# Three more feed-forward pairs by seven products, in another order of products, with other planned durations

## The chip, the core and the metric

The kernel runs on one core of one Trainium2 chip. The metric is the time of one execution in microseconds (us) on the device. A core has a matrix engine (TensorE, PE in the profile, with PEld for its weight loads), VectorE (DVE), ScalarE (ACT), GpSimd (POOL) and SyncE (SP). PE reads operands from the on-chip memory SBUF and writes sums into PSUM banks. VectorE and ScalarE take the sums out of PSUM again. SP and POOL only issue transfers (DMAs) here, apart from a few small fills by POOL.

## The reference, cut to what matters

The reference is a two-layer trunk over 512 tokens of width 1024. Each layer has a mixer (attention in layer 0, mLSTM in layer 1), a cross-attention to a memory of 256 rows, and a gated feed-forward network with a short convolution. The change touches the feed-forward network alone:

```python
def conv_ffn(xn, w_up, conv_w, conv_b, w_down):
    h = causal_depthwise_conv(xn @ w_up, conv_w) + conv_b
    g, u = jnp.split(h, 2, axis=-1)
    return (jax.nn.gelu(g) * u) @ w_down
```

`w_up` is 1024 x 5632 and `w_down` is 2816 x 1024. The convolution has three taps along the tokens. In front of it stands an RMS norm of x, and the result is added to x.

## The kernel before, in words

**Tiles.** x lies transposed, as 8 tiles of 128 channels x 512 tokens. All products are made of three fp32r matmuls: a value v is split into a high part (the cast to fp32r, on ScalarE) and a low part (v minus the high part, on VectorE), and `mm3` (line 265) adds high x high, high x low and low x high. So each weight tile that arrives costs one cast on ScalarE and one subtraction on VectorE (line 259, `sub`).

**The feed-forward network** is `ffn_steps` (line 1119). The 5632 output channels of `w_up` are 44 blocks of 128. Pair p (0 to 21) is gate block p with up block 22+p. There are two ways to compute a pair:

- `plain` (line 1291) does two blocks of 8 x 3 matmuls over 512 tokens, takes each out of PSUM while it scales by the norm (line 1300), and hands it to `tail`.
- `seven` (line 1310) treats the pair as a 2 x 2 product of halves: gate and up block, the two halves of the 1024 inputs, and the two halves of the tokens. Instead of eight quarter products it does seven (p1 to p7), each of 4 x 3 matmuls over 256 tokens, on sums of weight quarters and on sums of x quarters. The sums of x (`th`, `tl`) are formed once per layer by `forms` (line 1223). The sums of weights are made by an adding DMA of POOL (`onto`, line 1318, into the tile `sa`) and by two additions of VectorE (`b2` line 1343, `b4` line 1347). The outputs are combined by ScalarE (`v`, `c11`) and by VectorE (`u2`, `u3`, `c22`, `c12`, `c21`, all by line 1381), and then `scaled` (line 1402) multiplies by the norm.

`tail` (line 1247) does convolution (`conv` on ScalarE, line 1257, and four `tap`s on VectorE, line 1264), gelu (line 1272), the product of gate and up (line 1274) and the split of the result into `ah` and `al`.

`SEVEN` (line 26) names the pairs that go by seven products. They are 13 of 22, in both layers; 0 to 3, 5, 11, 16, 20 and 21 are plain.

**The down products.** The 22 pairs form chunks of 4, 4, 4, 4 and 6. When a chunk of four is done, its 8 down blocks (4 x 3 matmuls of 512 columns each) are put on a queue (lines 1431 to 1437). A plain pair takes up to two of them and a seven-product pair up to three, by `fill()`, until the queue is empty; pair 4 takes none. The last four blocks of chunk 3 come behind pair 21, and chunk 4 after them.

**The order of the work** is made when the program is built. `Sched` (line 139) is a list planner: each operation is a task with an engine, a planned duration, dependencies, a priority and buffers that it takes or frees. In `run` (line 161), among the tasks that can start soonest on their engine, the one with the lowest priority number is issued. A result counts as there for another engine `lat` after the task's planned end. The buffers of a name are handed out strictly in the order in which the tasks that take them were added (`want`, line 164). What comes out is a fixed order for each engine, and for the DMA queue of SP as well; on the chip each engine goes through its own order and waits where something is late. The planner's durations are the constants at lines 1126 to 1128 and the numbers in the calls: n columns cost `tt(n)` on VectorE and `act(n)` on ScalarE, `STT` is a tap, `ACV` a convolution start. A product counts 1.42 us and 0.7 us go to each three matmuls of 512 columns. Buffers of interest are `raw` (3 weight tiles as loaded), `sa` (3), `h` (3 split weight tiles), `hs` (2 rows of a pair before the convolution), `c` (1), and `u2`, `u3`, `v` (1 each).

A plain pair takes two `raw` tiles. A seven-product pair takes one, along with one `sa`, one `sb` and one `ra`.

Of the kernel before, what the change touches and what calls it, by code (L numbers as in the profile page):

```python
# [13 lines left out]
ALU = mybir.AluOpType  # L14
# [8 lines left out]
NPAIR = DFF // P  # L23
CHUNKS = [(0, 4), (4, 4), (8, 4), (12, 4), (16, 6)]

SEVEN = (4, 6, 7, 8, 9, 10, 12, 13, 14, 15, 17, 18, 19)
EPS = 1e-6

X_AT, X_STEP = 2.6, 0.6
# [30 lines left out]
class Plan:  # L60
# [11 lines left out]
    def add(self, fn, dur=0.0, deps=(), prio=None, take=(), free=(), chain=(), pre=(), after=0.0, order=(), load=(), st=None):  # L72
        it = Item(fn, dur, [d for d in deps if d is not None], len(self.items) if prio is None else prio, take, free, chain, pre, after, order, load, st)
        it.n = len(self.items)
        self.items.append(it)
        return it
# [62 lines left out]
class Sched:  # L139
# [5 lines left out]
        self.slots = {r: [0.0] * n for r, n in res.items()}  # L145
        self.turn = {r: 0 for r in res}

    def add(self, eng, dur, fn, deps, prio, take=(), free=(), lat=0.15):
        t = Task(eng, dur, fn, deps, prio, take, free, lat)
        t.n = len(self.tasks)  # L150
        self.tasks.append(t)
        return t
# [65 lines left out]
class Builder:  # L218
# [22 lines left out]
    def bank(self, tag):  # L241
        tag, bufs = BANKS[tag]
        return self.til(self.aux, tag, bufs=bufs)
# [875 lines left out]
    def ffn_steps(self, layer, mp):  # L1119
# [3 lines left out]
        nc, t = self.nc, self.t  # L1123
        sc = Sched(raw=3, h=3, s2=1, s4=1, a22=1, sa=3, sb=2, ra=2, hs=2, c=1, dr=2, v=1, u2=1, u3=1, act=10, acc=4, s=2, w=2)
        add = sc.add
        tt = lambda n: 0.14 + 1.06e-3 * n
        act = lambda n: 0.2 + 0.83e-3 * n
        ACV, STT = 0.81, 0.78
        clock = [0.0]
        state = {}  # L1130
        acts, acted = {}, {}
# [3 lines left out]
        def pe(dur, fn, deps, take=(), free=()):  # L1135
            clock[0] += dur
            return add("PE", dur, fn, deps, clock[0] - dur, take, free, 0.2)

        def joined(deps, prio, free):
            return add("-", 0.0, None, deps, prio, (), free, 0.0)  # L1140
# [52 lines left out]
        def norm():  # L1193
            prev = self.state
            st = {}
            n = {}

            def sums():
                n["ps"] = self.bank("s")
                for i in range(4):  # L1200
                    nc.tensor.matmul(n["ps"][:, 2 * i : 2 * i + 2], prev["sq"][:, i * P : (i + 1) * P], self.ones2[:], start=True, stop=True)

            def root():
                self.r = self.rsqrt(n["ps"], 4, 1.0 / DM, EPS)

            def spread():
                self.rb = self.bcast_cols(self.r, SEQ, self.sp, "rb", 1)

            a = pe(0.5, sums, (), [("s", st)])
            b = add("DVE", 2.3, root, [a], a.prio, (), [("s", st)])  # L1210
            s2 = {}
            c = pe(0.5, spread, [b], [("s", s2)], [("s", s2)])
            return add("ACT", 0.7, None, [c], c.prio)


        self.pad(mp, 192)
# [1 line left out]
        formed, pads = [], []  # L1218
# [65 lines left out]
        def rows(st, at):  # L1284
            def fn():
                st["hs_"] = hs2[st["_hs"]]

            return add("-", 0.0, fn, (), at, [("hs", st)])


        def plain(p, fill):
            st = {}
            at = clock[0]
            get = rows(st, at + 5.0)
            ready = []
            for j in range(2):
                b, last = block(t["up"][layer, 22 * j + p], KB8, own, clock[0], "acc", (), 2)

                def evac(j=j, b=b):
                    nc.vector.tensor_tensor(out=st["hs_"][:, j, 2:514], in0=b["ps"][:], in1=self.rb[:], op=ALU.mult)  # L1300

                if p == 0 and j == 0:
                    nonlocal normed
                    normed = norm()
                ready.append([add("DVE", 0.69, evac, [last, get, normed], clock[0] + 2.0, (), [("acc", b)])])
                fill()
            tail(p, st, ready, clock[0] + 3.0)


        def seven(p, fill):  # L1310
            st, sa, sb, r2, f1, f3, s2, s4, a22 = ({} for _ in range(9))
            at = clock[0]
# [35 lines left out]
            w22 = split(a22, 512, [l1], at + 4.0, lambda: small(a22, "a22"), [("a22", a22)], lambda: a22["ra"][:], [("ra", a22)])  # L1348
            w4 = split(s4, 512, [b4], at + 5.0, lambda: small(s4, "s4"), [("s4", s4)], SB, [("sb", sb)])
# [3 lines left out]
            def product(s, c, xh, xl, bank, first):  # L1353

                for k in range(4):
                    w = slice(c + k * P, c + (k + 1) * P)
                    self.mm3(st[bank][:, :256], s["wh"][:, w], s["wl"][:, w], xh(k), xl(k), first and k == 0, k == 3, True)

            X = lambda h, l: (lambda k: (self.xh, self.xl)[0][k + 4 * h][:, HALF[l]], lambda k: self.xl[k + 4 * h][:, HALF[l]])
            T = lambda i: (lambda k: th[k][:, 256 * i : 256 * i + 256], lambda k: tl[k][:, 256 * i : 256 * i + 256])  # L1360
            T1, T3, T2, T4 = (T(i) for i in range(4))
            bx, by, br, bv, bu2, bu3 = ({} for _ in range(6))
# [5 lines left out]
            n = 1.42  # L1368
            p1 = pe(n, lambda: opened("X", bx, "acc", f3, 0, *X(0, 0), "X", True), [w3], [("acc", bx)])
            p6 = pe(n, lambda: opened("Y", by, "acc", s2, 0, *T2, "Y", True), [w2, *formed], [("acc", by)], [("s2", s2)])  # L1370
            p5 = pe(n, lambda: opened("R", br, "s", f1, 512, *T1, "R", True), [w1], [("s", br)])
            get = rows(st, at + 2.0)
# [5 lines left out]
            def sum_(tag, out, a, b, op):  # L1378
                if tag:
                    st[tag] = self.til(mp, tag, (P, 256), bufs=1)  # L1380
                tt_(out=out(), in0=a(), in1=b(), op=op)

            bank = lambda n_: (lambda: st[n_][:, :256])
            tmp = lambda n_: (lambda: st[n_][:])
            hs = lambda j, l: (lambda: st["hs_"][:, j, 2 + 256 * l : 258 + 256 * l])
            v = add("ACT", act(256), v_, [p1], at + 1.5, [("v", bv)])
            u2 = add("DVE", 0.42, lambda: sum_("u2", tmp("u2"), bank("Y"), tmp("v_"), ALU.add), [p6, v], at + 4.0, [("u2", bu2)])
            p2 = pe(n, lambda: product(f3, 512, *X(1, 0), "X", False), [p1, v], (), [("h", f3)])
            c11 = add("ACT", act(256), lambda: nc.scalar.copy(hs(0, 0)(), bank("X")()), [p2, get], clock[0] + 2.0, (), [("acc", bx)])
            fill()  # L1390
            p7 = pe(n, lambda: product(f1, 0, *T3, "Y", False), [u2, p5], (), [("h", f1)])
            u3 = add("DVE", 0.42, lambda: sum_("u3", tmp("u3"), bank("Y"), tmp("v_"), ALU.add), [p7], clock[0], [("u3", bu3)])
            c22 = add("DVE", 0.42, lambda: sum_(None, hs(1, 1), tmp("u3"), bank("R"), ALU.subtract), [u3, p5, get], clock[0], (), [("u3", bu3)])
            fill()
            p4 = pe(n, lambda: product(a22, 0, *T4, "Y", False), [u3, w22], (), [("a22", a22)])
            p3 = pe(n, lambda: product(s4, 0, *X(1, 1), "R", False), [c22, w4], (), [("s4", s4)])
            c21 = add("DVE", 0.42, lambda: sum_(None, hs(1, 0), bank("Y"), tmp("v_"), ALU.add), [p4, get], clock[0], (), [("acc", by), ("v", bv)])
            c12 = add("DVE", 0.42, lambda: sum_(None, hs(0, 1), bank("R"), tmp("u2"), ALU.subtract), [p3, get], clock[0], (), [("s", br), ("u2", bu2)])

            def scaled():  # L1400
                h = st["hs_"][:, :, 2:514]
                tt_(out=h, in0=h, in1=self.rb[:].unsqueeze(1).to_broadcast([P, 2, 512]), op=ALU.mult)  # L1402

            m = add("DVE", 1.22, scaled, [c11, c22, c21, c12, normed], clock[0] + 2.0)
            fill()
            tail(p, st, [[m], [m]], clock[0] + 3.0)

# [1 line left out]
        xadded = [None] * 8  # L1409
        queue, late = [], []  # L1410

        def down(c, m, steps=1):
            first, nk = CHUNKS[c]
            d, last = block(
                t[f"down{c}"][layer, m], nk, lambda k: tuple(a[:] for a in acts[first + k]), clock[0], "w", [acted[first + k] for k in range(nk)], steps,
                "dr" if nk == 4 else "raw",
            )
            if m == 7:
                for k in range(nk):
                    joined([last], last.prio, [("act", acted[first + k].st)])  # L1420
            e = add("DVE", 0.69, lambda: self.xadd(m, d["ps"]), [last, xadded[m], *formed], clock[0] + 3.0, (), [("w", d)])
            xadded[m] = e
            return e

        def fill():
            nonlocal queue
            if queue:
                down(*queue.pop(0))

        normed = None  # L1430
        due = {4 * c + 5 + c // 3: c for c in range(4)}
        for p in range(22):
            if p in due:
                queue += [(due[p], m) for m in range(8)]
            if p == 19:
                queue, late = queue[:-4], queue[-4:]
            (seven if p in SEVEN else plain)(p, fill if p >= 5 else lambda: None)
            if p < 2:
# [5 lines left out]
        if layer == 0:  # L1444
            for m in range(8):
                e = down(4, m, 2)
                a = add("ACT", 1.43, lambda m=m: self.xprep(m, "mix", 1, state), [e], clock[0] + 3.0)
                add("DVE", 1.47, None, [a], clock[0] + 3.0)
        sc.run()
        if layer == 1:  # L1450
            self.finish(mp, *(list(p) for p in zip(*(acts[p] for p in range(16, 22)))))
# [364 lines left out]
```

## Time and profile before

| | us |
|---|---|
| median of 3 runs | 1508.07 |
| lowest and highest | 1508.01, 1509.43 |
| the profiled execution, its own time | 1509.76 |
| span from its first to its last instruction | 1508.0 |
| PE busy | 1493.6 |
| VectorE busy | 1172.4 |
| ScalarE busy | 791.5 |
| layer 0, first seven-product pair to last | 463.0 to 704.7 |
| layer 1, first seven-product pair to last | 1191.5 to 1433.0 |

The busy time of an engine is the union of the recorded times of its instructions. PE's matmuls are pipelined, so the recorded time of one (0.28 us for 256 columns) is longer than the distance to the next one's start, and that distance is what the stream costs. The same is true of VectorE and ScalarE. In a view of instructions in order of time, the first number is the start, the second the duration, then come the engine, the line and the tiles as out<-in. In the table by windows each engine has its busy time and, in brackets, the number of its instructions.

### The profile page before, as it was taken

Reading aid. Unit: us, or ns where it says so; the run is one execution under the profiler, and the core shown is the slowest. Engines: PE = TensorE matmul, PEld = TensorE weight load, DVE = VectorE, ACT = ScalarE, POOL = GpSimd, SP = SyncE. Lnnn points to the kernel's source line nnn. Section 1 sums busy time; section 2 is a strip of 40 time slices with the busy share of each in tenths; the row PEclk is TensorE's granted clock in tenths of the full one; section 3 lists DMA queues with packets and bytes.
Section 4 is the critical chain, followed back from the end, with each engine's and each line's share of the span. In section 5 each row is a group of like instructions: output and inputs, shape, how many; then the busy total and the mean of one; then the engine's idle time right before and its main releaser. Section 6 shows DMA issues by size and latency. Waiting matters only on the chain.

```text
span 1508.0 us, 22001 instructions
## 1 busy us (share of the span) xinstructions
PE 1493.6 (99%) x8314; PEld 1288.8 (85%) x8314; DVE 1172.4 (78%) x2191; ACT 791.5 (52%) x1322; POOL 61.4 (4%) x104
## 2 busy tenths in 40 slices
PE   9999999999999999999999999999999999999998
PEld 8888888888888999998888778888888899899987
DVE  6879885766588998988768857666657899899874
ACT  6767573444465454554446634444445555455444
POOL 2000120000000000000001000000000000000000
PEclk9999999999999999999999999999999999999999
DMA  5222223323246554622222222223323755464212
GB/s 179 85 71 72 91 96 121 113 84 112 85 138 182 156 148 132 155 84 83 81 97 84 75 94 86 98 100 108 112 85 119 189 147 148 125 158 117 91 58 76
DMA packets 58299, 167.02 MB, mean 111 GB/s; under 512 B 6480, under 2 KB 6480, under 8 KB 58192
## 3 DMA queue, kind: packets, MB, share of 16 engines
q1 hardware_dynamic: 53440, 150.86, 30.4%
q0 software_dynamic: 3744, 13.63, 5.3%
q8 instruction: 65, 1.06, 0.3%
q10 hardware_dynamic: 1008, 1.12, 0.2%
q14 instruction: 42, 0.34, 0.1%
HBM read 163.49 MB, written 2.10 MB: 110 GB/s over the span
## 4 chain that ended last, share of the span: by engine, by line
PE 91%; DVE 5%; DMA 2%; ACT 1%; issue 1%; DVEq 0%
PE acc L268 18%; PE acc L269 18%; PE acc L270 18%; PE w L268 5%; PE w L269 5%; PE w L270 5%; PE acc L329 3%; PE acc L330 3%; PE acc L331 3%; PE s L268 2%; PE s L270 2%; PE s L269 2%; DMA raw<-in_up_dram 1%; PE w L1604 1%; DVE wl L259 1%; PE w L681 1%
## 5 line engine op out<-in xcount | busy, mean ns | idle before, releaser
L268 PE MATMUL acc<-xh,wh 128*128 128x512 f32 (+1 forms) x880 | 325.3, 370 | 0.4 <-ACT v L1376 0.4
L270 PE MATMUL acc<-xh,wl 128*128 128x512 f32 (+1 forms) x880 | 321.0, 365 | 0.0
L269 PE MATMUL acc<-xl,wh 128*128 128x512 f32 (+1 forms) x880 | 320.8, 365 | 0.0
L259 DVE TENSOR_TENSOR wl<-raw,wh 128x1024 fp32r<-128x1024 f32 (+2 forms) x207 | 247.5, 1196 | 43.1 <-ACT wh L262 38.3
L262 ACT CAST wh<-raw 128x1024 fp32r<-128x1024 f32 (+2 forms) x137 | 140.9, 1030 | 169.8 <-PE acc L269 99.6
L268 PEld LDWEIGHTS acc<-xh,wh 128*128 128x128 f32 x880 | 165.7, 188 | 26.6 <-ACT v L1376 0.6
L270 PEld LDWEIGHTS acc<-xh,wl 128*128 128x128 f32 x880 | 165.6, 188 | 26.7
L269 PEld LDWEIGHTS acc<-xl,wh 128*128 128x128 f32 x880 | 165.8, 188 | 25.5
L1264 DVE SCALAR_TENSOR_TENSOR c<-hs,vec,c 128x512 f32<-128x512 f32 x176 | 127.4, 746 | 7.0 <-ACT c L1257 6.6
L269 PE MATMUL w<-al,wh 128*128 128x512 f32 x304 | 118.7, 390 | 0.0
L268 PE MATMUL w<-ah,wh 128*128 128x512 f32 x304 | 118.7, 390 | 0.0
L270 PE MATMUL w<-ah,wl 128*128 128x512 f32 x304 | 118.3, 389 | 0.0
L1257 ACT ACTIVATE c<-hs,vec 128x512 f32<-128x512 f32 x88 | 68.9, 811 | 47.4 <-DVE hs L1402 40.4
L1166 ACT CAST wh<-raw 128x1024 fp32r<-128x1024 f32 (+1 forms) x44 | 44.5, 1012 | 50.3 <-PE acc L269 26.4
L495 DVE TENSOR_TENSOR x<-w,x 128x512 f32<-128x512 f32 x72 | 49.5, 687 | 25.4 <-PE w L270 25.4
L270 PEld LDWEIGHTS w<-ah,wl 128*128 128x128 f32 x304 | 57.1, 188 | 12.1
L268 PEld LDWEIGHTS w<-ah,wh 128*128 128x128 f32 x304 | 57.1, 188 | 10.3
L269 PEld LDWEIGHTS w<-al,wh 128*128 128x128 f32 x304 | 57.2, 188 | 10.0
L1166 ACT CAST wh<-dr 128x512 fp32r<-128x512 f32 x64 | 39.5, 617 | 43.9 <-PE w L269 20.0
L330 PE MATMUL acc<-wl,xh 128*128 128x256 f32 (+1 forms) x192 | 62.0, 324 | 0.0
L329 PE MATMUL acc<-wh,xh 128*128 128x256 f32 (+1 forms) x192 | 62.0, 329 | 0.0
L331 PE MATMUL acc<-wh,xl 128*128 128x256 f32 (+1 forms) x192 | 61.9, 323 | 0.0
(373 smaller groups left out, 3598.7 us busy)
## 6 DMA issues: line engine op xcount, KB each, us to landing
raw<-in_up_dram SPq DMA_DIRECT2D x62, 512.0 KB, 3.2
dr<-in_down_dram SPq DMA_DIRECT2D x64, 256.0 KB, 2.7
sa<-in_up_dram SPq DMA_DIRECT2D x26, 512.0 KB, 4.1
sa<-in_up_dram POOLq DMA_DIRECT2D x26, 512.0 KB, 5.8
raw<-in_xk_dram SPq DMA_DIRECT2D x16, 512.0 KB, 3.3
raw<-in_wo_dram SPq DMA_DIRECT2D x16, 512.0 KB, 3.2
raw<-in_xq_dram SPq DMA_DIRECT2D x16, 512.0 KB, 3.2
raw<-in_xv_dram SPq DMA_DIRECT2D x16, 512.0 KB, 3.2
```

The lines of the kernel that those rows point to most:

```text
L259: self.nc.vector.tensor_tensor(out=lo, in0=v, in1=hi.bitcast(F32), op=ALU.subtract)
L262: self.nc.scalar.copy(hi, v)
L268: mm(out, wh, xh, start=first, stop=False, skip_group_check=parts)
L269: mm(out, wh, xl, start=False, stop=False, skip_group_check=parts)
L270: mm(out, wl, xh, start=False, stop=last, skip_group_check=parts)
L329: mm(ps, xh[k][:, ts], wh[:, ws], start=(k == 0), stop=False)
L330: mm(ps, xh[k][:, ts], wl[:, ws], start=False, stop=False)
L331: mm(ps, xl[k][:, ts], wh[:, ws], start=False, stop=(k == 7))
L495: self.nc.vector.tensor_tensor(out=self.x[m][:], in0=ps[:], in1=self.x[m][:], op=ALU.add)
L1166: nc.scalar.copy(st["wh"][:, :cols], st[tag][:, :cols])
L1257: nc.scalar.activation(st["c_"][:, j, :], hs()[:, j, 2:514], AF.Identity, scale=self.col("cw", (layer * 3 + 2) * 44 + blk), bias=self.col( ...
L1264: nc.vector.scalar_tensor_tensor(out=c, in0=hs()[:, j, n : n + 512], scalar=w, in1=c, op0=ALU.mult, op1=ALU.add)
```

## The change

`SEVEN` gains the pairs 5, 11 and 20, so that 16 of 22 pairs go by seven products, in both layers. The planner's durations for VectorE and ScalarE become smaller and the latency behind a task of these engines larger. In `seven` the products come in another order: p7 directly behind p2, then p3 and p4; the places of the three `fill()` calls move with them. No operation of a pair is another one than before.

```diff
-SEVEN = (4, 6, 7, 8, 9, 10, 12, 13, 14, 15, 17, 18, 19)
+SEVEN = (4, 5, 6, 7, 8, 9, 10, 11, 12, 13, 14, 15, 17, 18, 19, 20)
...
-    def add(self, eng, dur, fn, deps, prio, take=(), free=(), lat=0.15):
+    def add(self, eng, dur, fn, deps, prio, take=(), free=(), lat=0.25):
...
-        tt = lambda n: 0.14 + 1.06e-3 * n
-        act = lambda n: 0.2 + 0.83e-3 * n
-        ACV, STT = 0.81, 0.78
+        tt = lambda n: 0.055 + 1.06e-3 * n
+        act = lambda n: 0.1 + 0.83e-3 * n
+        ACV, STT = 0.71, 0.66
...
             c11 = add("ACT", act(256), lambda: nc.scalar.copy(hs(0, 0)(), bank("X")()), [p2, get], clock[0] + 2.0, (), [("acc", bx)])
+            p7 = pe(n, lambda: product(f1, 0, *T3, "Y", False), [u2, p5], (), [("h", f1)])
+            u3 = add("DVE", 0.34, lambda: sum_("u3", tmp("u3"), bank("Y"), tmp("v_"), ALU.add), [p7], clock[0], [("u3", bu3)])
+            c22 = add("DVE", 0.34, lambda: sum_(None, hs(1, 1), tmp("u3"), bank("R"), ALU.subtract), [u3, p5, get], clock[0], (), [("u3", bu3)])
             fill()
-            p7 = pe(n, lambda: product(f1, 0, *T3, "Y", False), [u2, p5], (), [("h", f1)])
-            u3 = ...
-            c22 = ...
+            p3 = pe(n, lambda: product(s4, 0, *X(1, 1), "R", False), [c22, w4], (), [("s4", s4)])
+            c12 = add("DVE", 0.34, lambda: sum_(None, hs(0, 1), bank("R"), tmp("u2"), ALU.subtract), [p3, get], clock[0], (), [("s", br), ("u2", bu2)])
+            p4 = pe(n, lambda: product(a22, 0, *T4, "Y", False), [u3, w22], (), [("a22", a22)])
+            c21 = add("DVE", 0.34, lambda: sum_(None, hs(1, 0), bank("Y"), tmp("v_"), ALU.add), [p4, get], clock[0], (), [("acc", by), ("v", bv)])
             fill()
-            p4 = ...
-            p3 = ...
-            c21 = ...
-            c12 = ...
```

The other edits give smaller planned durations to single tasks: the evacuation of a block 0.69 to 0.6, `u2` and the other sums of 256 columns 0.42 to 0.34, `scaled` 1.22 to 1.14, the norm's root 2.3 to 2.1 and its broadcast 0.7 to 0.52, and at the end of layer 0 the preparation of x for layer 1 from 1.43 and 1.47 to 1.2 and 1.3.

More of the change, by code (lines that the diff above doesn't have):

```diff
@@ L1209, in norm @@
             a = pe(0.5, sums, (), [("s", st)])
-            b = add("DVE", 2.3, root, [a], a.prio, (), [("s", st)])
+            b = add("DVE", 2.1, root, [a], a.prio, (), [("s", st)])
             s2 = {}
             c = pe(0.5, spread, [b], [("s", s2)], [("s", s2)])
-            return add("ACT", 0.7, None, [c], c.prio)
+            return add("ACT", 0.52, None, [c], c.prio)
         self.pad(mp, 192)
@@ L1304, in plain @@
                     normed = norm()
-                ready.append([add("DVE", 0.69, evac, [last, get, normed], clock[0] + 2.0, (), [("acc", b)])])
+                ready.append([add("DVE", 0.6, evac, [last, get, normed], clock[0] + 2.0, (), [("acc", b)])])
                 fill()
@@ L1386, in seven @@
             v = add("ACT", act(256), v_, [p1], at + 1.5, [("v", bv)])
-            u2 = add("DVE", 0.42, lambda: sum_("u2", tmp("u2"), bank("Y"), tmp("v_"), ALU.add), [p6, v], at + 4.0, [("u2", bu2)])
+            u2 = add("DVE", 0.34, lambda: sum_("u2", tmp("u2"), bank("Y"), tmp("v_"), ALU.add), [p6, v], at + 4.0, [("u2", bu2)])
             p2 = pe(n, lambda: product(f3, 512, *X(1, 0), "X", False), [p1, v], (), [("h", f3)])
             c11 = add("ACT", act(256), lambda: nc.scalar.copy(hs(0, 0)(), bank("X")()), [p2, get], clock[0] + 2.0, (), [("acc", bx)])
+            p7 = pe(n, lambda: product(f1, 0, *T3, "Y", False), [u2, p5], (), [("h", f1)])
+            u3 = add("DVE", 0.34, lambda: sum_("u3", tmp("u3"), bank("Y"), tmp("v_"), ALU.add), [p7], clock[0], [("u3", bu3)])
+            c22 = add("DVE", 0.34, lambda: sum_(None, hs(1, 1), tmp("u3"), bank("R"), ALU.subtract), [u3, p5, get], clock[0], (), [("u3", bu3)])
             fill()
-            p7 = pe(n, lambda: product(f1, 0, *T3, "Y", False), [u2, p5], (), [("h", f1)])
-            u3 = add("DVE", 0.42, lambda: sum_("u3", tmp("u3"), bank("Y"), tmp("v_"), ALU.add), [p7], clock[0], [("u3", bu3)])
-            c22 = add("DVE", 0.42, lambda: sum_(None, hs(1, 1), tmp("u3"), bank("R"), ALU.subtract), [u3, p5, get], clock[0], (), [("u3", bu3)])
+            p3 = pe(n, lambda: product(s4, 0, *X(1, 1), "R", False), [c22, w4], (), [("s4", s4)])
+            c12 = add("DVE", 0.34, lambda: sum_(None, hs(0, 1), bank("R"), tmp("u2"), ALU.subtract), [p3, get], clock[0], (), [("s", br), ("u2", bu2)])
+            p4 = pe(n, lambda: product(a22, 0, *T4, "Y", False), [u3, w22], (), [("a22", a22)])
+            c21 = add("DVE", 0.34, lambda: sum_(None, hs(1, 0), bank("Y"), tmp("v_"), ALU.add), [p4, get], clock[0], (), [("acc", by), ("v", bv)])
             fill()
[L1395 to L1398, printed above, removed]
             def scaled():
@@ L1402, in scaled @@
                 tt_(out=h, in0=h, in1=self.rb[:].unsqueeze(1).to_broadcast([P, 2, 512]), op=ALU.mult)
-            m = add("DVE", 1.22, scaled, [c11, c22, c21, c12, normed], clock[0] + 2.0)
+            m = add("DVE", 1.14, scaled, [c11, c22, c21, c12, normed], clock[0] + 2.0)
             fill()
@@ L1420, in down @@
                     joined([last], last.prio, [("act", acted[first + k].st)])
-            e = add("DVE", 0.69, lambda: self.xadd(m, d["ps"]), [last, xadded[m], *formed], clock[0] + 3.0, (), [("w", d)])
+            e = add("DVE", 0.6, lambda: self.xadd(m, d["ps"]), [last, xadded[m], *formed], clock[0] + 3.0, (), [("w", d)])
             xadded[m] = e
@@ L1446, in ffn_steps @@
                 e = down(4, m, 2)
-                a = add("ACT", 1.43, lambda m=m: self.xprep(m, "mix", 1, state), [e], clock[0] + 3.0)
-                add("DVE", 1.47, None, [a], clock[0] + 3.0)
+                a = add("ACT", 1.2, lambda m=m: self.xprep(m, "mix", 1, state), [e], clock[0] + 3.0)
+                add("DVE", 1.3, None, [a], clock[0] + 3.0)
         sc.run()
```

## The prediction

> **What bounds the kernel now.** I read the page's engine rows first, then PE's waits, then the feed-forward stretches by windows, and the chain of waits where PE stops.
>
> ```profile
> span 1508.0 us, 22001 instructions
> ...
> PE 1493.6 (99%) x8314; PEld 1288.8 (85%) x8314; DVE 1172.4 (78%) x2191; ACT 791.5 (52%) x1322; POOL 61.4 (4%) x104
> ```
>
> PE is busy 99%. PE's waits by line show how little of the feed-forward time is waiting:
>
> ```profile
> PE acc L268 <- DVE u L1381: 2.6, 2, 1.7
> ...
> PE acc L268 <- ACT v L1376: 0.4, 1, 0.4
> ```
>
> In the seven-product code PE waits 3.0 us in both layers together. So fewer matmuls are a gain, as long as the other engines can follow. How near they are, by windows (VectorE is the third engine column):
>
> ```profile
> 463.00:491.00 28.00, 26.33 (x156) 23.07 (x155) 23.93 (x37) 13.49 (x20) 1.72 (x2) 1.00 0.57 158
> 491.00:509.00 18.00, 18.00 (x122) 16.55 (x121) 16.68 (x26) 9.04 (x14) 0.85 (x1) 1.00 0.61 163
> 527.00:555.00 28.00, 28.00 (x207) 26.51 (x206) 27.39 (x44) 15.92 (x25) 1.73 (x2) 1.00 0.60 153
> 704.70:724.00 19.30, 19.30 (x87) 15.99 (x86) 15.59 (x23) 9.29 (x14) 0.00 (x0) 1.00 0.16 48
> ```
>
> VectorE is the engine to watch: from 527 to 555 it is busy 27.39 of 28 us and PE still never stops. ScalarE has half its time free. The one real stop, at pair 4 of layer 0, in the chain of waits:
>
> ```profile
> 465.87 9.22 DMA raw<-in_up_dram
> ...
> 475.22 0.69 DVE sb L1341
> 475.91 0.60 DVE s2l L259
> 476.51 0.60 DVE al L259
> 477.12 0.34 DVE u L1381
> 477.46 0.04 issue
> 477.51 0.38 PE acc L268
> ```
>
> A weight tile for pair 6 lands late. VectorE, which works in order, waits 3.47 us for it with `u3` of pair 4 queued behind, and p4 waits for `u3`. Layer 1 has the same at 1203 to 1206.
>
> **Part 1: three pairs per layer go by seven products.** What a matmul costs PE is the distance of starts:
>
> ```profile
> 480.05 0.28 PE L268 MATMUL s<-xh,s4h 128*128 128x256 f32 x1
> 480.17 0.28 PE L269 MATMUL s<-xl,s4h 128*128 128x256 f32 x1
> ...
> 480.41 0.40 PE L268 MATMUL w<-ah,wh 128*128 128x512 f32 x1
> 480.64 0.40 PE L269 MATMUL w<-al,wh 128*128 128x512 f32 x1
> ```
>
> That is about 0.117 us for 256 columns and 0.227 for 512. By whole stretches: plain pair 16, with no fill in it, runs from 650.72 to 661.63, 10.91 us for 48 matmuls, so a down block of 12 is 2.73. Pair 6 with three fills starts at 491.31 and the next pair at 509.36: 18.05 - 3 x 2.73 = 9.86. Pairs 8 and 9 run 11 products without a fill from 527.41 to 542.75: 1.395 each, 9.76 for seven. One exchanged pair saves 10.91 - 9.86 = 1.05 us (1.15 at best). Three pairs in two layers: **6 x 1.05 = 6.3 us off PE**.
>
> The Trainium skill ("TensorE: Matmul & The Clock Gate", section "Back-to-back issue gap") gives the warm gap as N / 2.4 + 2.5 ns, 109 ns for 256 and 216 for 512; by it a pair would save 48 x 0.216 - 84 x 0.109 = 1.2 us and six 7.2. The trace's 117 and 227 ns disagree, and I keep them.
>
> **Part 2: the order of products.** Each change between 256 and 512 columns costs a little: 18.05 - 9.76 - 8.19 = 0.10 us over three visits to a fill, about 0.035 each. Now p7 follows p2 and two fills stand together behind p4, so a pair with three fills has two visits. Seven such pairs per layer: 14 x 0.035 = **0.5 us**. It also frees f1's split tile one fill (2.73 us) earlier, for the next weight. p3 now waits for `u3` and `c22` in a row (2 x 0.34 us and the way to PE), which the fill between covers. Without a fill (pairs 4, 8, 12, 17, 20) the next pair's p1 (1.4 us) covers it; if both are missing, it costs at most about 1 us.
>
> **Part 3: the planner's durations.** They move no work, they only reorder. Do they fit? Back-to-back starts on VectorE:
>
> ```profile
> 484.49 0.74 DVE L1264 SCALAR_TENSOR_TENSOR c<-hs,vec,c 128x512 f32<-128x512 f32 x1
> 485.15 0.68 DVE L495 TENSOR_TENSOR x<-w,x 128x512 f32<-128x512 f32 x1
> 485.75 0.74 DVE L1264 SCALAR_TENSOR_TENSOR c<-hs,vec,c 128x512 f32<-128x512 f32 x1
> 486.41 1.22 DVE L259 TENSOR_TENSOR wl<-raw,wh 128x1024 fp32r<-128x1024 f32 x1
> 487.55 1.53 DVE L1264 SCALAR_TENSOR_TENSOR c<-hs,vec,c 128x512 f32<-128x512 f32 x2
> ```
>
> A tap of 0.74 us is followed after 0.66, an addition of 0.68 after 0.60, a subtraction of 1.22 after 1.14. The new constants (0.66, 0.60, 1.14) are these distances, and 0.60 + 0.25 of latency is what 0.68 + 0.15 was. Cost taken: 0; the old plan had VectorE too slow, by 13%, and the slack that this left in the order goes. Bounds: a better order could take off the 3.0 us of waits, a tighter one could add as much.
>
> **Does VectorE follow?** By distances, a seven-product pair costs it five halves of 0.60, two weight subtractions of 1.14, five sums of 0.335, `scaled` 1.14, four taps of 0.66 and two ends of 0.60: 11.9 us, against 9.8 on PE. A plain pair costs 2 x 1.14 + 2 x 0.60 + 2.64 + 1.2 = 7.3 against 10.9; a fill 1.2 against 2.73. A chunk of four pairs with 8 fills:
>
> - before (one plain): PE 62.2, VectorE 52.6, 85%
> - after (four by seven): PE 61.0, VectorE 57.2, 94%
> - pairs 4 to 8, five by seven with 8 fills: PE 70.8, VectorE 69.1, 98%
> - pairs 16 to 21, 4 fills: PE 71.9, VectorE 67.0, 93%
>
> So the cover holds over each stretch, but is thin in pairs 4 to 8: PE can draw fills forward when products wait, and 527 to 555 shows VectorE 98% busy with PE running. There I expect PE to lose some 1.5 us per layer, as now. The old stop should go for its own reason: as a plain pair, 5 takes two `raw` tiles, so pair 6's load gets pair 4's tile (free at 463.5) and is issued last of a crowd. Now pair 5's load is next behind pair 4's and gets a tile free at 451.9. Minus 3.0, plus 3.0: **0**. Should the cover fail, the first rival has the price.
>
> **Sum.** 6.3 + 0.5 = 6.8 us less. The profiled execution took 1509.76 (span 1508.0, 1.76 around it), 1.69 over the median of the runs; against itself it would become 1503.0, and the median 1508.07 becomes **1501.3**.
>
> **The rivals.**
>
> 1. *VectorE starves PE in pairs 4 to 8* (slower). If it loses a share w of its time to waits at the head of its queue, the stretch lasts 69.1 / (1 - w) instead of 70.8. The gain of 3.4 per layer is gone at 69.1 / 74.2, w = 7%. At w = 10% it lasts 76.8: 2 x (6.0 - 3.4) = +5.2, **1513**. For it: from 463 to 491 VectorE idles 4.07 of 28 us. Against: 3.47 of that is the late load that should go, and 527 to 555 idles 2%. Chance 0.13.
> 2. *Durations are what VectorE pays*: the old constants were right, 0.68 and 1.22 are occupied in full. A seven-product pair is then 13.5 and a fill 1.37; pairs 4 to 8 need 78.5 against 70.8, 9 to 12 65.0 against 61.0, 17 to 21 some 6 more than PE: 16 to 18 per layer, **1535**. The starts above (0.60 behind an addition of 0.68) speak against it. Chance 0.04. The Trainium skill has such a rule ("VectorE: DVE Perf Modes", section "The DRAIN you can't avoid"): the next operation doesn't start until the pipe is empty; the starts in this trace disagree.
> 3. *Loads land late again*, once for each added pair: more traffic (1.8 MB against 1.0 for a pair, from lists of 512 and 256 KB) into a crowd such as 467 to 473, where DMA is busy throughout. Six times the mean stop of 1.3 us is 7.8, which eats the gain: **1509**. For it: 9.2 us to landing where 3.2 is usual. Against: between 491 and 573 no load was late at 155 GB/s. Chance 0.15.
> 4. *All goes*: the stops vanish and none comes: 1501.3 - 3.0 = **1498.3**. Chance 0.18.
>
> That the planner issues products in other than the written order costs at most the 0.5 of part 2.
>
> **How the numbers follow.** The forecast (1499 to 1505) has 0.50. The measurement tells 0.2% (3.0 us) from no change: faster is below 1505.05, slower above 1511.1. Faster: 0.50 + 0.18 + 0.04 of rival 3 = 0.72. Same: 0.08 of rival 3. Slower: 0.03 of rival 3, 0.13, 0.04 = 0.20. The range reaches from rival 4 less its 0.1 us more per pair and some more (1496.5) to rival 3's upper part (1510); it leaves out rivals 1 and 2.
>
> **What would show it.** Right: PE has 8314 + 6 x 36 = 8530 matmuls and about 6 to 7 us less busy time; its waits in lines 268 to 270 stay near 3 us; the VectorE wait for `raw` at L1341 near 470 is gone; VectorE is over 95% busy from 463 to 534. Wrong: PE waits of many us for `wl`, `s2l` or `u` in pairs 4 to 8 or 17 to 20 (rival 1), starts on VectorE as far apart as durations (2), waits for `raw` or `sa` at L1341 (3), or a stop behind pair 21, where the last `al` must be ready within the 10.9 us of four late fills.

## The result, and the profile after

| | before | after |
|---|---|---|
| median of the runs, us | 1508.75 | 1498.60 |
| lowest and highest, us | 1508.01, 1510.11 | 1498.12, 1500.39 |
| the profiled execution, its own time | 1509.76 | 1498.12 |
| span | 1508.0 | 1496.3 |
| layer 0, from the first product of pair 4 to the last matmul of pair 21 | 260.8 | 256.5 |
| layer 1, the same | 260.6 | 255.3 |

After to before is 0.9934, with a 95% interval of 0.9917 to 0.9951. The change is 10.2 us faster. The two stretches of the table, which are what the change touches, are 9.6 us shorter together. The spans of the two profiled executions differ by 11.7, of which 1.76 lie ahead of pair 4 of layer 0, where both do the same work: from 20 to 40 us the granted clock was 0.86 in the one and 0.93 in the other.

The page's first lines after:

```profile
span 1496.3 us, 22561 instructions
...
PE 1485.1 (99%) x8530; PEld 1291.6 (86%) x8530; DVE 1194.5 (80%) x2245; ACT 806.1 (54%) x1352; POOL 67.1 (4%) x110
```

There are 216 matmuls more, as many as six exchanged pairs bring, and 8.5 us less PE time, since a matmul of 256 columns takes about half of one of 512 (1.2 of the 8.5 lie ahead of the first feed-forward network). Of PE's waits in lines 268 to 270 one is left in the list (before: 3.0 us in three):

```profile
PE s L268 <- DVE hs L1381: 0.6, 1, 0.6
```

By windows, where VectorE is the third engine column:

```profile
463.00:491.00 28.00, 28.00 (x209) 26.56 (x208) 27.97 (x45) 16.32 (x28) 1.72 (x2) 1.00 0.75 192
491.00:509.00 18.00, 18.00 (x122) 16.55 (x121) 17.98 (x30) 9.41 (x17) 0.86 (x1) 1.00 0.53 134
527.00:555.00 28.00, 28.00 (x207) 26.41 (x206) 27.42 (x45) 15.73 (x25) 1.73 (x2) 1.00 0.65 168
```

From 463 to 491 PE now works all 28.00 us instead of 26.33, and VectorE does 45 operations where it did 37. It is busy throughout, and still PE doesn't wait.

Where the old stop was, the addition into `sb` (line 1341) tells more than the prediction saw. It runs once in each seven-product pair. Before, on VectorE:

```profile
459.11 0.68 DVE L1341 TENSOR_TENSOR sb<-sa,raw 128x512 f32<-128x512 f32 x1
...
470.46 0.69 DVE L1341 TENSOR_TENSOR sb<-sa,raw 128x512 f32<-128x512 f32 x1 [0.39 <-issue]
...
475.22 0.69 DVE L1341 TENSOR_TENSOR sb<-sa,raw 128x512 f32<-128x512 f32 x1 [3.47 <-DMA raw<-in_up_dram]
```

The first is pair 4's. Pair 5 is plain and has none, so the second is pair 6's and the third, which waits 3.47 us, is pair 7's. The tile that landed too late was pair 7's, not pair 6's. After:

```profile
471.68 0.67 DVE L259 TENSOR_TENSOR wl<-dr,wh 128x512 fp32r<-128x512 f32 x1
472.28 0.67 DVE L1341 TENSOR_TENSOR sb<-sa,raw 128x512 f32<-128x512 f32 x1
```

This is the third addition again, now pair 6's (4, 5, 6), and it follows the operation before it without a gap. The SP queue says why. Its issues of `raw` tiles, with the time to landing and the pair (the tiles are handed out in the pairs' order, two to a plain pair and one to a seven-product pair; the semaphores that the casts of pairs 4 and 5 wait for agree):

```
before: 440.2 (3.2) pair 4   443.9 (3.1), 451.9 (6.5) pair 5   463.5 (6.8) pair 6   465.9 (9.2) pair 7
after:  438.4 (3.3) pair 4   442.2 (3.4) pair 5   450.1 (6.4) pair 6   463.5 (6.3) pair 7   469.4 (4.3) pair 8
```

Before, pair 6's load went out at 463.5, when pair 4 gave its tile back, and pair 7's at 465.9, when pair 5 gave back its first; pair 7's addition, queued ahead of `u3` of pair 4, waited for it until 475.1. After, with one tile less for pair 5, pair 6's load goes out at 450.1 and is there 15.7 us ahead of its use. Pair 7's lands at 469.8, and its addition comes at 493.27. It can't stand in front of `u3` of pair 4 (470.42) any more: there are two `sb` tiles, and pair 5 now has the one that pair 7 needs until 475.

### The profile page after: what moved, and what is told of

It is laid out like the page before. It is cut to its first block, busy times and chain, and to the rows that moved or that the text cites. A ratio compares the mean times of both kernels' runs of the same rounds, so it can differ in the third digit from the quotient of the medians.

```text
span 1496.3 us, 22561 instructions
## 1 busy us (share of the span) xinstructions
PE 1485.1 (99%) x8530; PEld 1291.6 (86%) x8530; DVE 1194.5 (80%) x2245; ACT 806.1 (54%) x1352; POOL 67.1 (4%) x110
## 4 chain that ended last, share of the span: by engine, by line
PE 93%; DVE 3%; ACT 1%; issue 1%; DMA 1%; DVEq 0%; ACTq 0%
PE acc L268 18%; PE acc L269 18%; PE acc L270 18%; PE w L269 5%; PE w L268 5%; PE w L270 5%; PE acc L329 3%; PE acc L330 3%; PE acc L331 3%; PE s L268 2%; PE s L270 2%; PE s L269 2%; PE w L1604 1%; PE w L681 1%; PE s L395 1%
## 5 line engine op out<-in xcount | busy, mean ns | idle before, releaser
L268 PE MATMUL acc<-xh,wh 128*128 128x512 f32 (+1 forms) x832 | 301.1, 362 | 0.0
L270 PE MATMUL acc<-xh,wl 128*128 128x512 f32 (+1 forms) x832 | 297.2, 357 | 0.0
L269 PE MATMUL acc<-xl,wh 128*128 128x512 f32 (+1 forms) x832 | 296.8, 357 | 0.0
L259 DVE TENSOR_TENSOR wl<-raw,wh 128x1024 fp32r<-128x1024 f32 (+2 forms) x201 | 240.7, 1198 | 42.3 <-ACT wh L262 38.3
L270 PEld LDWEIGHTS acc<-xh,wl 128*128 128x128 f32 x832 | 156.7, 188 | 22.9
L268 PEld LDWEIGHTS acc<-xh,wh 128*128 128x128 f32 x832 | 156.8, 188 | 22.3
L269 PEld LDWEIGHTS acc<-xl,wh 128*128 128x128 f32 x832 | 156.8, 188 | 22.1
L268 PEld LDWEIGHTS w<-ah,wh 128*128 128x128 f32 x304 | 57.1, 188 | 10.2
L495 DVE TENSOR_TENSOR x<-w,x 128x512 f32<-128x512 f32 x72 | 49.3, 684 | 15.7 <-PE w L270 15.7
L268 PE MATMUL acc<-mem,wh 128*128 128x256 f32 (+1 forms) x192 | 61.5, 320 | 0.0
L269 PE MATMUL acc<-mem,wh 128*128 128x256 f32 (+1 forms) x192 | 61.1, 318 | 0.0
```

What stands on the lines that cost most here:

```text
L259: self.nc.vector.tensor_tensor(out=lo, in0=v, in1=hi.bitcast(F32), op=ALU.subtract)
L268: mm(out, wh, xh, start=first, stop=False, skip_group_check=parts)
L269: mm(out, wh, xl, start=False, stop=False, skip_group_check=parts)
L270: mm(out, wl, xh, start=False, stop=last, skip_group_check=parts)
L495: self.nc.vector.tensor_tensor(out=self.x[m][:], in0=ps[:], in1=self.x[m][:], op=ALU.add)
```

## The experiments

All were compared with the kernel before on the same chip. *Stretch* is the sum over both layers of the stretch of the first table. *Gaps* is what the starts of PE's matmuls in it lie apart beyond the usual (0.115 us for 256 columns, 0.227 for 512, where the distance is over 0.16 or 0.28). Both come from the one profiled execution of each kernel.

| | pairs | durations | order | median | ratio, 95% interval | stretch | gaps |
|---|---|---|---|---|---|---|---|
| before (with the change) | 13 | old | old | 1508.75 | | 521.4 | 4.0 |
| the change | 16 | new | new | 1498.60 | 0.9934, 0.9917 to 0.9951 | 511.8 | 2.7 |
| e1 | 16 | old | old | 1501.24 | 0.9947, 0.9935 to 0.9958 | 513.2 | 2.3 |
| e2 | 13 | new | old | 1512.01 | 1.0023, 1.0011 to 1.0034 | 519.8 | 2.6 |
| e3 | 13 | old | new | 1512.99 | 1.0027, 1.0017 to 1.0037 | 526.6 | 10.3 |
| e4 | 13 | new | new | 1513.88 | 1.0035, 1.0022 to 1.0049 | 524.0 | 8.3 |
| e5 | 16 | new | old | 1498.51 | 0.9924, 0.9911 to 0.9937 | 511.1 | 0.2 |
| e6 | 16 | old | new | 1501.09 | 0.9941, 0.9928 to 0.9954 | 513.5 | 4.7 |
| e7, pair 5 added | 14 | old | old | 1503.55 | 0.9959, 0.9945 to 0.9973 | 516.4 | 1.2 |
| e8, pair 11 added | 14 | old | old | 1508.69 | 0.9992, 0.9982 to 1.0002 | 520.7 | 5.4 |
| e9, 0.6 us more VectorE work per pair | 16 | new | new | 1499.77 | 0.9939, 0.9924 to 0.9953 | 511.4 | 1.1 |
| e10, 1.2 us more | 16 | new | new | 1506.39 | 0.9987, 0.9977 to 0.9996 | 518.7 | 7.2 |
| e11, p4 before p3 | 16 | new | its own | 1497.57 | 0.9927, 0.9914 to 0.9940 | 510.4 | 0.0 |
| e12, pair 16 added | 17 | new | old | 1497.17 | 0.9920, 0.9907 to 0.9933 | 509.0 | 0.3 |

The kernel before stood at medians of 1508.68 with e1 to e4, 1509.70 with e5 to e8 and 1508.28 with e9 to e12. So a difference between medians of two groups, or of one and the change, can be off by 1 us or so; the stretch is the finer measure for these.

**e1, the 16 pairs alone.**

```diff
-SEVEN = (4, 6, 7, 8, 9, 10, 12, 13, 14, 15, 17, 18, 19)
+SEVEN = (4, 5, 6, 7, 8, 9, 10, 11, 12, 13, 14, 15, 17, 18, 19, 20)
```

> The kernel before with SEVEN alone widened to 16 pairs; order of products and planned durations stay old. Theory A (the matmuls and pair 5 do it): six pairs save 1.15 us each, 6.9, and since pair 5 now takes one raw tile the two late loads for pair 6 go, another 1 to 3: 1499 to 1501. Theory B (the planned durations are what keeps VectorE in step): with durations 13% too long the order is wrong for pairs 4 to 8, PE waits there for wl, s2l or u by several us per layer: 1503 or more.

Measured: 1501.24, 7.4 us less and 0.24 above the upper end of theory A. The exchange alone brings most of the gain, and the theory that the planned durations make it falls. What they add is a smaller part: with them (e5) the gaps go from 2.3 to 0.2 us and the median to 1498.51. In e1 they are short waits of p4 for `u3`, 0.17 us in the longest that the profile names, at the pairs without a fill.

**e2, the durations alone**, and **e3, the order alone**, with 13 pairs. The edits are those of the change, without the rest of it.

> The kernel before with the new planned durations and latencies alone; 13 pairs by seven products, old order of products. Theory A: PE's work is the same, the late loads for pair 6 stay since pair 5 is still plain: within 1 us of before. Theory B: the stops of 3.0 us go: 1505 to 1506.

> The kernel before with the new order of products alone. Theory A: 0.07 us for each of 26 pairs by less changing between 256 and 512 columns, some 1.5 us: 1506.5 to 1507.5, the stop at pair 4 stays or moves to p3, which now comes first and waits for u3 and c22. Theory B: no gain from the order itself, 1508 to 1509.

Measured: 3.3 and 4.3 us more than before. No theory had that; theory A of e3 had named the move of the stop to p3, but put no price on it. In e3 the load for pair 7 is late again (the third addition of the layer), and the new order makes it dearer. VectorE at that place in e3:

```profile
474.25 0.69 DVE L1341 TENSOR_TENSOR sb<-sa,raw 128x512 f32<-128x512 f32 x1 [4.32 <-DMA raw<-in_up_dram]
...
476.07 0.42 DVE L1381 TENSOR_TENSOR u<-acc,v 128x256 f32<-128x256 f32 x1
476.40 0.68 DVE L1347 TENSOR_TENSOR sb<-sb,raw 128x512 f32<-128x512 f32 x1
477.00 0.41 DVE L1381 TENSOR_TENSOR hs<-u,s 128x256 f32<-128x256 f32 x1
```

p4 could go on behind `u3` at 476.07; p3, which now stands first, also needs `c22` at 477.00. And a stop so long changes the clock. PE by windows in e3; the third column from the end is the granted clock:

```profile
474.00:477.40 3.40, 0.33 (x2) 0.00 (x0) 3.15 (x7) 0.62 (x1) 0.00 (x0) 0.98 0.01 5
477.40:480.00 2.60, 2.53 (x12) 2.54 (x13) 2.35 (x4) 0.00 (x0) 0.00 (x0) 0.50 0.20 43
480.00:483.00 3.00, 3.00 (x20) 2.80 (x20) 2.09 (x5) 1.24 (x2) 0.00 (x0) 0.89 0.65 225
```

After a wait of 3.1 us PE is granted half its clock for some 3.4 us: all of the second row (2.6 us), and what the 0.98 and the 0.89 stand for in its neighbours. Before, a wait of 1.7 us at the same place left it at 1.00, and so did one of 1.92 at 1206 in layer 1 of e3. But the wait need not be one. In e4 PE waited 1.73 us, did three matmuls, and waited 0.93, and then:

```profile
1203.60:1207.00 3.40, 3.40 (x18) 3.40 (x17) 2.15 (x4) 0.00 (x0) 0.00 (x0) 0.50 0.46 158
```

The Trainium skill ("TensorE: Matmul & The Clock Gate", section "HAM oscillation — how this bites in real kernels") warns of idle gaps over about 3.4 us. Here 3.1 us between the recorded end of one matmul and the next start was enough (starts lay 3.5 us apart), and in e4 two shorter waits were.

For e2 the profile gives less than the runs: its profiled execution took 1508.19 and has a shorter stretch than before, while its 12 runs reach from 1507.57 to 1515.33. What the slower ones paid isn't in a profile. Each run's mean granted clock is on record: 0.997 in the run of 1507.57, 0.995 and 0.994 in those of 1515.19 and 1515.33. So the slower ones had less clock, and further stops like those of e3 and e4 would fit; it isn't shown. The runs of e3, e4 and e8 spread by 3.4 to 6.5 us too, those of the kernels with pair 5 by seven products by 1.8 to 3.8.

**e4, durations and order with 13 pairs.** The change with the old `SEVEN`.

> The changed kernel with the old 13 pairs: durations and order new. Theory A: the order's 1.5 us and perhaps some of the stops, 1506 to 1507.5. Theory B: stops gone and order: 1504 to 1505.

Measured: 5.1 us more than before. So two of the three parts, each alone or together, are a loss without the third. There is a late load in each layer again (VectorE waits 2.45 and 2.99 us, here ahead of pair 6's addition). The profiled execution, 1510.90, was the fastest of e4's six, so its stretch shows less than the median does.

**e5 and e6, the 16 pairs with one of the other two parts.** The change, e5 with the old block of products and e6 with the old durations.

> The changed kernel with the old order of products: 16 pairs, new durations. Theory A: as the changed kernel without the order's 1.2 to 1.5 us: 1499.5 to 1500.5. If instead p7 behind p2 is what feeds pairs without a fill, PE waits in pairs 4, 8, 12, 17 and 20: over 1502.

> The changed kernel with the old durations: 16 pairs, new order of products. Theory A: 1498 to 1500, as the changed kernel. Theory B (durations keep VectorE in step): PE waits in pairs 4 to 8, 1502 or more.

Measured: 1498.51 and 1501.09. e5 is 1 us faster than theory A had it and as fast as the change, so with 16 pairs the order gives nothing in the end. e6 differs from the change in the durations alone. It is 2.5 us slower by the medians, with overlapping intervals, and 1.7 by the stretch. Theory A expected 1498 to 1500 for e6 and missed it by 1.1; theory B had 1502 or more with waits in pairs 4 to 8, and the two longest stops, 0.95 us each, are at 667 and 1391, where p3 waits for `c22`.

**e7, pair 5 alone, and e8, pair 11 alone.**

```diff
 e7: SEVEN = (4, 5, 6, 7, 8, 9, 10, 12, 13, 14, 15, 17, 18, 19)
 e8: SEVEN = (4, 6, 7, 8, 9, 10, 11, 12, 13, 14, 15, 17, 18, 19)
```

> The kernel before with pair 5 alone added to SEVEN. Theory A (the ring of raw tiles): 2 x 1.15 = 2.3 us of matmuls and the two stops at pair 4 behind the late load of pair 6's raw tile (1.8 and 1.1 us on PE) gone: 1503.0 to 1504.5, and no wait of VectorE for raw at the addition into sb near 470. Rival (the stop is a matter of the traffic at the start of the seven-product pairs, whoever asks for it): 1506.5, with a wait of 3 us or more at the same place.

> The kernel before with pair 11 alone added to SEVEN. Both theories: 2 x 1.15 us of matmuls and nothing else, the stops at pair 4 stay: 1506 to 1506.8. If a run of four pairs by seven products starves PE by VectorE, the gain is less.

Measured: 6.2 us less with pair 5, as theory A had it, 1.0 less with pair 11 (its interval reaches 1.0002; the forecast for e8 was about 2 to 3 less). The matmuls saved are the same: the stretches without their gaps are 2.2 and 2.0 us shorter. But the gaps fall from 4.0 to 1.2 us in e7 and rise to 5.4 in e8. What else pair 5 brings is the rings of `raw` and `sb` tiles. The waits ahead of the addition into `sb`, e7 and then e8:

```profile
  DMA raw<-in_up_dram: 0.2, 1
```

```profile
  issue: 4.1, 2
  DMA raw<-in_up_dram: 3.3, 1
  DMA sa<-in_up_dram: 0.5, 1
```

The longest single gaps of VectorE ahead of that addition, near pairs 4 and 5 of the two layers, in us: before 3.47 and 3.02; e2 1.95 and 2.32; e3 4.32 and 3.27; e4 2.45 and 2.99; e8 3.31 and 3.65. In the change and in e1, e5, e6, e7, e9 to e12 there is none over 0.6. All five kernels with a plain pair 5 wait there for a late load (pair 7's in before, e3 and e8, pair 6's in e2 and e4), and none of the others does. The rival, that the crowd of loads makes the wait whoever asks, falls. Its crowd is still there: in e7 the load issued at 465.2 takes 8.7 us, but it is pair 7's, whose addition now comes at 495.0, and pair 6's tile is there since 458.8. How much of this the `raw` tiles do and how much the `sb` tiles isn't separated.

**e9 and e10, how much room VectorE has.** A low part that is computed already is computed once more, in each seven-product pair:

```diff
+                lo = lambda: self.sub(s["wl"][:, :cols], raw(), s["wh"][:, :cols])
+                if s is s4:                      # e10: s is s4 or s is a22
+                    h = add("DVE", tt(cols), lo, [h], due - 2.0)
-                return add("DVE", tt(cols), lambda: self.sub(...), [h], due - 2.0, (), free)
+                return add("DVE", tt(cols), lo, [h], due - 2.0, (), free)
```

> The changed kernel with one VectorE subtraction of 512 columns (s4's low part) done twice in each seven-product pair, known to the planner: 0.60 us more VectorE work per pair, the same result, no other work. If VectorE's cover is as thin as the sum has it (pairs 4 to 8: 72.1 us of VectorE against 70.7 of PE), 1.5 us per layer are lost: 1501 to 1502. If fills drawn forward and loads made early give more room, nothing: within 1 us of the changed kernel, 1498 to 1499.5. If VectorE were paid by durations (0.68 per such operation, 13.5 per pair), it would already be the bound and 16 pairs x 0.68 x 2 layers would show in full: 1520.

> As the run with one subtraction more, with two of them in each pair (s4's and a22's): 1.2 us more per pair. By the sum pairs 4 to 8 need 75.1 against 70.7, 9 to 12 62.0 against 60.9: 5.6 us per layer, 1509 to 1511, with VectorE busy throughout and PE waiting for weights in pairs 4 to 12. If there is room beyond the sum, less than half of it: under 1504.

Measured: 1499.77 and 1506.39. Against the change the first costs 1.2 us by the medians, inside the intervals and 0.3 above what was expected, and nothing in the stretch; the second 7.8 and 6.9. e10 by windows:

```profile
463.00:491.00 28.00, 28.00 (x205) 26.36 (x205) 28.00 (x46) 15.43 (x26) 2.13 (x3) 1.00 0.72 184
491.00:534.00 43.00, 43.00 (x312) 40.50 (x311) 42.81 (x71) 22.32 (x35) 2.59 (x3) 1.00 0.58 147
534.00:595.00 61.00, 60.06 (x413) 55.12 (x412) 59.84 (x96) 32.94 (x52) 3.45 (x4) 1.00 0.57 154
```

In pairs 4 to 8 PE is still busy throughout, with VectorE busy 70.81 of 71 us; it loses in the pairs behind, once the room is used up. So the sum (5.6 us per layer) was about 60% too dear, and the room lies between 0.6 and 1.2 us per pair. That an operation is paid by its duration falls with e9: it would already have been the bound.

**e11, p4 before p3.**

```diff
+            p4, c21 = ...
             p3, c12 = ...
-            p4, c21 = ...
             fill()
```

> The changed kernel with p4 in front of p3 (p7 still right behind p2, the fills as in the change). The theory that the order's gain of 0.6 ns on each matmul of 256 columns is given back by p3's wait for c22: the waits of 2.7 us at the products go and the gain of 1.6 us stays: 1496 to 1497.5. If the waits come from VectorE's load instead, no change: 1498 to 1499.

Measured: 1497.57, no gap left at all, the stretch 1.4 us shorter than the change's and 0.7 shorter than e5's. The theory holds, with half of its size: a matmul of 256 columns costs 116.3 ns in the change, 116.8 in e5 and 116.6 here. The traces show where the rest went. From its first matmul to the next product, p7 takes 1.413 us directly behind a fill and 1.379 behind p2; p4 takes 1.416 behind a fill and 1.379 behind p3; p3 takes 1.41 behind either. Of 32 pairs, p7 stands behind a fill in 22 in e5, and in 8 here and in the change. p4 stands behind one in 22 of e5 and in 24 here, but in the change it mostly follows p3. So e11 keeps p7's part, 14 x 0.034 = 0.5 us, and gives up p4's, 22 x 0.037 = 0.8. In whole runs e11, e5 and the change aren't told apart.

**e12, pair 16 by seven products too.**

```diff
-SEVEN = (4, 5, 6, 7, 8, 9, 10, 11, 12, 13, 14, 15, 17, 18, 19, 20)
+SEVEN = (4, 5, 6, 7, 8, 9, 10, 11, 12, 13, 14, 15, 16, 17, 18, 19, 20)
```

> The kernel with new durations and old order of products, and pair 16 by seven products too (17 pairs, 4 to 20). 2 x 1.15 us of matmuls less than with 16: 1496 if VectorE still follows. By the sum pairs 13 to 16 need 57.2 on VectorE against 61.0, 17 to 21 71.6 with the four late fills against 70.7 with 16's slack gone: if that binds, the gain is eaten, 1498 to 1500, with waits behind pair 17.

Measured: 1497.17, the stretch 2.1 us shorter than that of e5, from which it differs by pair 16 alone, with gaps of 0.3 us. VectorE follows here as well. It is the fastest kernel of the study by its median; its interval overlaps the change's.

## Why the prediction was right, and where its sizes were off

**What bounds it, and the direction.** Right: PE's work set the time, and less of it shortened it. The forecast was 6.8 us less, 10.2 were measured. That is inside the range, but 1498.60 lies just below the forecast's own 1499 to 1505. In the two stretches, without their gaps, the exchange saves 6.4 us in the old order (before to e5, 517.3 to 510.9), the new order another 1.8 (e5 to the change, 509.1), and the gaps fall by 1.3 (4.0 to 2.7): 9.6 together. The forecast had 6.3, 0.5 and 0. So the exchange was sized rightly, and what fell short was the order and the waits.

**Part 1, the exchange.** Right: 1.05 us per pair was forecast, and six pairs save 6.4 us, 1.07 each. Pair 10 in e5, which has the old order and three fills, by the starts of its first product and of the next pair's:

```profile
550.84 0.28 PE L268 MATMUL acc<-xh,wh 128*128 128x256 f32 x1
...
568.89 0.28 PE L268 MATMUL acc<-xh,wh 128*128 128x256 f32 x1
```

That is 18.05 us, what pair 6 took before. In the change the same pair takes less, and the difference is the order's:

```profile
550.20 0.28 PE L268 MATMUL acc<-xh,wh 128*128 128x256 f32 x1
...
568.15 0.28 PE L268 MATMUL acc<-xh,wh 128*128 128x256 f32 x1
```

17.95 - 3 x 2.73 = 9.76, the value of the stretch without a fill.

**Part 2, the order.** Forecast 0.5, for one visit to a fill less in 14 pairs at 0.035 us. p7's part is just that (14 x 0.034, e11). The forecast left out p4, which now follows p3 instead of a fill in most pairs and is 0.037 us shorter each time (e11). The matmuls of 256 columns went from 116.8 ns to 116.3, and with 2688 of them that is some 1.4 us. It is not the number of changes between 256 and 512 columns that counts, as the forecast had it, but which product stands behind the fill: p3 takes as long there as elsewhere. But the gain is given back. The step that I covered by the fill, p3's wait for `u3` and `c22`, isn't covered everywhere. The longest gap of the change, 0.76 us at 665, is p3 waiting for `c22`. A short one is at 606, where PE does five matmuls of p4, then p3, and then the rest of p4. p3 starts 0.23 us behind the matmul before it instead of 0.115, when `c22` (on VectorE from 605.85, for 0.41) is there:

```profile
606.08 0.28 PE L269 MATMUL acc<-tl,a22h 128*128 128x256 f32 x1
606.31 0.39 PE L268 MATMUL s<-xh,s4h 128*128 128x256 f32 x1
```

The gaps of the change (2.7 us, against 0.2 in e5) eat the gain; e5 is as fast. e11 has no gaps and keeps p7's share of the gain.

**Part 3, the durations.** Cost 0 was taken. The reading behind it, that VectorE is paid by distances of starts, holds by e9. The size is off: with 16 pairs they are worth 2.1 us in the stretch and 2.7 in the medians (e1 to e5). With 13 pairs the median is 3.3 us worse with them (e2).

**"Minus 3.0, plus 3.0: 0".** This is the other term that made the forecast too small. The minus came (3.0 of recorded idle time, 4.0 by the starts), and pair 5 is what brings it (e7 against e8). But the reading behind it was one pair off. The load that gets pair 4's tile at 463.5 is pair 6's, and it landed in time to cost 0.39 us. The one that cost 3.47 us was pair 7's, in the tile that pair 5 gave back at 465.8. It is gone because each later load has a tile earlier and because pair 7's addition now needs the `sb` tile that pair 5 has, and so leaves `u3` of pair 4 free, which the prediction hadn't seen.

By the medians pair 5 is worth 6.2 - 2.3 = 3.9 us beyond its matmuls (e7), more than the 2.8 us of gaps that its profile has less. Runs of the kernel before that lost clock as in e3 would explain the rest, but this isn't shown. The plus came in part: gaps of 2.7 us are left, by p3's waits and a load that is late by 1.96 us at 628, and all but 0.2 of them not in pairs 4 to 8, where I had put them. What 98% of VectorE means was read too darkly: PE takes fills forward, VectorE does 0.6 us more per pair without loss, and only at 1.2 more is the gain gone.

**The rivals.** Rival 4 (1498.3, chance 0.18) has the time that came, but by luck in part: in the change 2.7 of 4.0 us of gaps are left, and the order's larger gain makes up for them. Its mechanism is that of e5 and e11, with gaps of 0.2 and 0.0. Rival 1, VectorE starving PE, has a real mechanism, but its point lies some 5 to 10% of VectorE's work away, and the first to suffer are the pairs behind 8 (e10). Rival 2 fell by e9. Rival 3, loads late once for each added pair, fell: e1 and e5, with the same 16 pairs, have no wait for a load at the addition at all. The two such waits of the change, 1.96 us at 628 and 1.05 at 644 in layer 0, come with the order of products (e6 and e11 have one each as well).

## What to carry to other kernels

Before a plain stage is exchanged for one with fewer matmuls, count per stage what the next engine pays by distances of starts, and then ask what the exchange does to the rings of buffers: a stage that takes one load tile less lets the loads behind it start earlier. Parts of a change that were made for each other need not be gains alone: here two of three are losses without the third. Put last the product that waits for the longer chain on another engine (e11 against the change).

## What the runs showed of the hardware

- The granted clock fell to 0.50 for some 3.4 us behind one PE wait of 3.1 us (e3), and for as long behind two of 1.73 and 0.93 us with three matmuls between them (e4). It stayed at 1.00 behind single ones of 1.7 us (before) and 1.92 (e3). So a late load can cost more than its wait.
- VectorE ran 70.81 of 71 us busy (e10, 463 to 534) with PE busy all the time. A full engine beside the bound isn't a bound as long as its work can be done ahead.
- A product of twelve matmuls of 256 columns took 1.36 to 1.43 us by which product it was and what stood before it. p7 took 1.413 behind matmuls of 512 columns and 1.379 behind p2; p3 took 1.41 either way. Why isn't shown.
